# A fused hybrid trunk on one core: scan products of a chunk issued as one burst, squares of the head summed by TensorE, eight early conditioning products

## The chip, the cores and the metric

The kernel runs on one core of one Trainium2 chip. The metric is device time in microseconds (us), the median of several executions; lower is better. The engines are called as in the profile: PE (TensorE, matrix products), PEld (its weight loads), DVE (VectorE), ACT (ScalarE), POOL (GpSimd) and SP (SyncE, which only issues DMAs). Each engine works through its own queue in order, as the kernel's schedule has written it.

## The reference, cut to what matters

One layer over 1024 time steps and 1024 channels, in fp32. `u` is the modulated RMSNorm of the input; the modulation comes from the conditioning vector `c`. One projection of `u` feeds a gated short convolution and a state-space (SSD) mixer with 8 groups of 4 heads; both are merged by gates, followed by an MLP.

```python
mod = (c_act @ w_ada[i] + b_ada[i]).reshape(bsz, N_MOD, D_MODEL)[:, :, None, :]
u = rms_norm(x, ln1[i]) * (1.0 + scale1) + shift1          # rms_norm: x * rsqrt(mean(x*x) + EPS) * w
gl, cb, cc, cx, z, xbc, dt = split(u @ w_in)
xbc = silu(causal_depthwise_conv(xbc, ssm_conv_w) + ssm_conv_b)   # width 4
xs, bs, cs = split(xbc)
# scan over chunks, per group (4 heads share bs and cs):
scores = einsum('btgn,bsgn->btsg', cq, bq)
y_diag = einsum('btsg,btsgr,bsgrp->btgrp', scores, decay, xq)
y_off = einsum('btgn,bgrpn->btgrp', cq, state) * exp(a_cum)[..., None]
new_state = state * exp(a_cum[:, -1])[..., None, None] + einsum('bsgn,bsgr,bsgrp->bgrpn', bq, to_end, xq)
y = (y + d_skip * xs) * silu(z)                             # then a norm per group
x = x + gate1 * (merged @ w_o);  x = x + gate2 * (square(relu(u2 @ w_up)) @ w_down)
```

## The kernel before

Every product in fp32 precision is made of three products of split operands: the high part of the weight with the high and the low part of the activations, and the low part with the high part. A tile of a projection (128 channels by 1024 steps) is `proj`: 8 blocks of 128 inputs by two halves by three products, 48 products of 128x512. Four PSUM banks (`mm`) hold the outputs, so two such tiles at a time.

The order of the work on each engine is set when the kernel is built: a scheduler takes the instructions in the order in which the Python code issues them and moves them by its own estimate of times and by dependencies. `tc.issue_after(x)` adds a dependency of order: what is issued under it stands behind `x`. In the head (the first 105 us or so) the order is pinned to that of the code.

The stages:

- **Head** (0 to about 105 us). The input arrives in two halves of 512 steps (`h` = 0, 1), eight blocks `k` each. `square(h, k)` squares a block on ACT and adds it on DVE to an accumulator (`accs`, tile `sacc`; the squares are `ssq`). `sums(h)` sums over the partitions: for each of four 128-step columns, one product of the accumulator with a column of ones into `st`. A product here is an fp32 one, which PE runs in two passes. `root` turns the sums into 1/sqrt on DVE, `spread` brings that to all partitions with another product. Between these PE works on the first tiles of the projection (`part`, line L402, tiles `mm`, `sx`, `st`).
- **Early projections** (about 105 to 640 us). Conditioning products run on DVE: `gemv` multiplies a 512 KB block of `w_ada` (tile `wv`, loaded by POOL's queue) by the conditioning and sums it (line L323, result `mcol`). `gemvs(n, ...)` does the next n of 32. Ten stand ahead of the projections, three stand ahead of each of the two pairs f = 12 and 14 of the gate tiles, and the others in later loops up to the z tiles. `strassen_pair` (L155 products) does pairs of projection tiles by a Strassen scheme; ACT copies its first result out of PSUM (`cu`, L178).
- **Scan** (about 640 to 1300 us). Eight groups of eight chunks of 128 steps. While `ssd_group(g)` runs its chunks, `proj_group(g+1)` supplies four tiles of the next group: two of `xs`, one of `bf`, one of `cf`. Lines L121, L122 and L124 are their products. `xbc_evac` takes a tile out of PSUM: two copies on ACT into one of two padded tiles (`raw0`, `raw1`, L738), a scaled copy on ACT into `cacc` (L740), three shifted multiply-adds on DVE that read `raw` (the taps of the convolution), tanh on ACT (L743), and a last multiply-add on DVE.
- **Output projections and MLP** (1300 us to the end), which the change does not touch.

One chunk c of the scan has these products on PE:

- **A**: the scores of `cf` and `bf` (L779) and three transposes (L780 to L782). DVE makes `smk` (masked scores), `xd` and `xe` from it.
- **B**: four heads of `xd` times `seg`, in tiles of 64 columns (L802). `seg` is the masked decay: four relus and one exp on ACT from `acb` (a DMA of 256 KB by SP's queue, L777, two buffers), times `smk` on DVE.
- **O**: two products of the state with `cf` into the same PSUM tile (L807), not in chunk 0.
- **C**: the update of the state from `bt` and `xe` (L824), not in the last chunk. DVE adds it to the decayed state.

DVE then scales O (`t`) and adds B, and adds the skip term into `xs` (two multiply-adds of 128x128 a chunk). A has two PSUM tiles, B and C one each. After the last chunk of a group, `xs` is multiplied by the gate (`zs`, two operations of 128x1024), and `finish` squares and sums these for the group's norm.

Of the kernel before, what the change touches and what calls it, by code (L numbers as in the profile page):

```python
# [16 lines left out]
P = 128  # L17
# [21 lines left out]
def hybrid_trunk(tc, xT, par, hrows, crow, wada1, wadak, wada2, win, wdt, wco, wso, wo, wup, wdt_, wdn, out):  # L39
# [3 lines left out]
    def tt(o, a, b, op, eng=dve):  # L43
        return eng.tensor_tensor(out=o, in0=a, in1=b, op=op)  # L44
# [296 lines left out]
    accs = {}  # L341

    def square(h, k):
        sq = p0.tile([P, H], F32, name="ssq" if k else "sacc", bufs=2 if k else 1)
        act.activation(sq, xt[k][h], AF.Square)
        if k:
            tt(accs[h], accs[h], sq, ALU.add)
        else:
            accs[h] = sq

    def scale_of(j):
        stt(s1c[:, j:j + 1], mcol[:, 8 + j:9 + j], 1.0, prm[:, LN1 + j:LN1 + j + 1], ALU.add, ALU.mult)

    st = ps0.tile([P, H], F32, name="st")

    def sums(h):
        for j in range(4):
            pe.matmul(st[:, 4 * h + j:4 * h + j + 1], lhsT=accs[h][:, j * P:j * P + P], rhs=ones[:, 0:1],
                      start=h == j == 0, stop=True, skip_group_check=True)

    def root(h):
        r = rsqrt_eps(p0, st[:, 4 * h:4 * h + 4], 1.0 / T, [P, 4], "nst")
# [55 lines left out]
    for h in (0, 1):  # L418
        act.activation(ct[:, hs[h]], rows_c[h], AF.Tanh, scale=0.5)
        stt(cb[:, hs[h]], ct[:, hs[h]], 1.0, rows_c[h], ALU.add, ALU.mult)  # L420
    sums(0)
    first_col()
    high(0)
    high(1)
# [14 lines left out]
    for j in range(1, KT):  # L439
        scale_col(j)  # L440
        shift_lo(j - 1, 0)
        if j == 1:
            for i in (0, 1, 2):
                part((0,), (0, 1), 0, (i,))
            part((0,), (2,), 0, (0, 1))
        scaled(j, 0)
        gemv(wa[j, 0], j)
        if j == 1:
            load_ada(3)
            low(2)  # L450
            part((0,), (2,), 0, (2,))
            load_f(5)
        if j > 2:
            for k in {3: (0, 1, 2), 4: (3, 4), 5: (5, 6), 6: (7,), 7: ()}[j]:
                square(1, k)
        shift_hi(j, 0)
        if j == 1:
            high(3)
            part((0,), (3,), 0, (0, 1))
            high(4)  # L460
        if j == 2:
            load_ada(4)
            part((1,), range(3), 0)
            part((1,), (3,), 0, (0, 1))
            low(3)
            part((0, 1), (3,), 0, (2,))
            part((0, 1), (4,), 0, (0, 1))
            load_f(6)
            high(5)
        if j == 3:  # L470
            load_ada(5)
            part((2,), range(4), 0)
            part((2,), (4,), 0, (0, 1))
            low(4)
            part((0, 1, 2), (4,), 0, (2,))
            part((0, 1, 2), (5,), 0, (0, 1))
            load_f(7)
        if j == 4:
            load_ada(6)
            part((3,), range(5), 0)  # L480
            part((3,), (5,), 0, (0, 1))
            low(5)
            part((0, 1, 2, 3), (5,), 0, (2,))
            high(6)
            low_by_dma(6)
        if j == 5:
            load_ada(7)
            part((4,), range(6), 0)
            part((0, 1, 2, 3, 4), (6,), 0, (0, 1))
            high(7)  # L490
            low_by_dma(7)
        if j == 6:
            part((5,), range(6), 0)
            sums(1)
            part((5,), (6,), 0, (0, 1))
            part((0, 1, 2, 3, 4, 5), (6,), 0, (2,))
        if j == 7:
            dg = root(1)
            part((6,), range(7), 0)
            keep_rb(spread(dg))  # L500
# [51 lines left out]

    p0d = tc.alloc_tile_pool(name="p0d", bufs=1, reuse_waits="tile")
    p0g = tc.alloc_tile_pool(name="p0g", bufs=1, reuse_waits="tile")
    gemvs(10, p0g, 3)
    wdr = p0d.tile([P, KT, NH], F32, name="wdr")
    sp.dma_start(wdr, wdt)
    wd = p0d.tile([P, KT, 2 * NH], F32R, name="wd")
# [67 lines left out]
    for f in range(8, 16, 2):  # L626
        ts_ = [glp.tile([P, T], F32, name="glt") for _ in (0, 1)]

        def gl_ev(i, h, src):
            act.activation(ts_[i][:, hs[h]], src, AF.Tanh, scale=0.5)  # L630

        if f == 10:
            dt_chain()
        elif f > 10:
            gemvs(3, pe1)
        strassen_pair(pe1, win[f], win[f + 1], X, gl_ev)
        for i in (0, 1):
            act.dma_start(gl_d[f + i], ts_[i])
# [133 lines left out]
    def ssd_group(g, xs, bf, cf, prev):  # L772
        state = None
        for c in range(NC_):
            cs = slice(c * P, c * P + P)
            acb = p2.tile([P, 4, P], F32, name="acb")
            sp.dma_start(acb, ac_d[4 * g:4 * g + 4, cs].partition_broadcast(P))  # L777
            A = psA.tile([P, 512], F32, name="A")
            pe.matmul(A[:, 0:P], lhsT=bf[:, cs], rhs=cf[:, cs], start=True, stop=True)  # L779
            pe.transpose(A[:, 128:256], xs[:, 0, cs], ident)  # L780
            pe.transpose(A[:, 256:384], xs[:, 1, cs], ident)
            pe.transpose(A[:, 384:512], bf[:, cs], ident)  # L782
            smk = p2.tile([P, P], F32, name="smk")
            tt(smk, A[:, 0:P], tri, ALU.mult)
            xd = p2.tile([P, 4, 64], F32, name="xd")
            xq = A[:, 128:384].rearrange("p (r k) -> p r k", r=4)
            tt(xd, xq, dt_t[:, c, 4 * g:4 * g + 4].unsqueeze(2).broadcast_to([P, 4, 64]), ALU.mult)
            if c < NC_ - 1:
                bt = p2.tile([P, P], F32, name="bt")
                act.copy(bt, A[:, 384:512])  # L790
                xe = p2.tile([P, 4, 64], F32, name="xe")
                tt(xe, xq, de_t[:, c, 4 * g:4 * g + 4].unsqueeze(2).broadcast_to([P, 4, 64]), ALU.mult)
            seg = p2.tile([P, 4, P], F32, name="seg")
            for r in range(4):
                hd = 4 * g + r
                act.activation(seg[:, r, :], acb[:, r, :], AF.Relu, bias=acum[:, c, hd:hd + 1], scale=-1.0)
            act.activation(seg, seg, AF.Exp, scale=-1.0)
            tt(seg, seg, smk.unsqueeze(1).broadcast_to([P, 4, P]), ALU.mult)
            Bk = psB.tile([P, 512], F32, name="B")
            for r in range(4):  # L800
                o = 64 * (r % 2)
                pe.matmul(Bk[o:o + 64, P * (r // 2):P * (r // 2) + P], lhsT=xd[:, r, :], rhs=seg[:, r, :],  # L802
                          start=True, stop=True, skip_group_check=True)
            ydv = Bk[:, 0:256].rearrange("p (q t) -> p q t", q=2)
            if c > 0:
                for q in (0, 1):
                    pe.matmul(Bk[:, 256 + P * q:256 + P * q + P],  # L807
                              lhsT=state[:, 2 * q:2 * q + 2, :].rearrange("p r k -> p (r k)"),
                              rhs=cf[:, cs], start=True, stop=True, skip_group_check=True)
                ebc = p2.tile([P, 2, P], F32, name="ebc")  # L810
                for q in (0, 1):
                    act.activation(ebc[64 * q:64 * q + 64], acb[64 * q:64 * q + 64, q::2, :], AF.Exp)
                t1 = p2.tile([P, 2, P], F32, name="t1")
                tt(t1, Bk[:, 256:512].rearrange("p (q t) -> p q t", q=2), ebc, ALU.mult)
                tt(t1, ydv, t1, ALU.add)
                src = t1
            else:
                src = ydv
            for q in (0, 1):
                col = DSK + 2 * g + q  # L820
                stt(xs[:, q, cs], xs[:, q, cs], prm[:, col:col + 1], src[:, q, :], ALU.mult, ALU.add)
            if c < NC_ - 1:
                C = psC.tile([P, H], F32, name="C")[:, 0:256]
                last = pe.matmul(C, lhsT=bt, rhs=xe.rearrange("p r k -> p (r k)"), start=True, stop=True)  # L824
                ns = p2.tile([P, 4, 64], F32, name="state")
                cv = C.rearrange("p (r k) -> p r k", r=4)
                if c == 0:
                    dve.tensor_copy(ns, cv)
                else:
                    tt(ns, state, edec[:, c, 4 * g:4 * g + 4].unsqueeze(2).broadcast_to([P, 4, 64]), ALU.mult)  # L830
                    tt(ns, cv, ns, ALU.add)
                state = ns
            if c == 4 and prev is not None:
                finish(prev, last)
            if c == 5:
                zs = [p2.tile([P, T], F32, name="zs") for _ in (0, 1)]
                for q in (0, 1):
                    sp.dma_start(zs[q], z_d[2 * g + q])
            if c == 6 and g in (5, 7):
                rstd(*{5: (0, 4), 7: (4, 6)}[g])  # L840
            yield
        for q in (0, 1):
            tt(zs[q], xs[:, q, :], zs[q], ALU.mult)
            pool.dma_start(y_d[2 * g + q], zs[q])
        return g, zs
# [422 lines left out]
```

## Time and profile before

| what | value |
|---|---|
| time, median of 3 runs | 2101.52 us (2098.99 to 2104.03) |
| time of the profiled execution | 2104.39 us |
| its span | 2102.6 us |
| PE, DVE, ACT busy over the span | 98%, 71%, 46% |
| head 0 to 105 us: PE busy, granted clock | 95.18 us, 0.93 |
| 105 to 640 us: PE busy of 535 | 528.87 us, clock 1.00 |
| scan 640 to 1300 us: PE, DVE, ACT busy of 660 | 653.11, 482.55, 387.86 us, clock 1.00 |
| 1300 us to the end: PE busy of 802.6 | 790.09 us, clock 0.99 |

In the rows of the timeline the columns are start, duration, engine, line and operation, output and inputs, shapes, count, and in brackets the idle time ahead of it with what ended it. Rows of successive matmuls overlap, since a matmul's end lies behind the start of the next: the time that one takes from the stream is read from start to start. In the groups, after the first bar stand the busy time in us and the mean of one in ns, after the second the idle time of that engine ahead of them and what ended most of it. In the rows of windows stand the window, its length, the busy time of PE, PEld, DVE, ACT and POOL with counts, the granted clock of PE, the share of the DMA engines and GB/s.

### The profile page before, as it was taken

Reading aid. Unit: us, or ns where it says so; the run is one execution under the profiler, and the core shown is the slowest. Engines: PE = TensorE matmul, PEld = TensorE weight load, DVE = VectorE, ACT = ScalarE, POOL = GpSimd, SP = SyncE. Lnnn points to the kernel's source line nnn. Section 1 sums busy time; section 2 is a strip of 40 time slices with the busy share of each in tenths; the row PEclk is TensorE's granted clock in tenths of the full one; section 3 lists DMA queues with packets and bytes.
Section 4 is the critical chain, followed back from the end, with each engine's and each line's share of the span. In section 5 each row is a group of like instructions: output and inputs, shape, how many; then the busy total and the mean of one; then the engine's idle time right before and its main releaser. Section 6 shows DMA issues by size and latency. Waiting matters only on the chain.

```text
span 2102.6 us, 26286 instructions
## 1 busy us (share of the span) xinstructions
PE 2067.2 (98%) x9736; PEld 1693.4 (81%) x9736; DVE 1491.5 (71%) x2348; ACT 962.1 (46%) x1570; POOL 178.2 (8%) x247
## 2 busy tenths in 40 slices
PE   8999999999999999999999999999999999999997
PEld 6878878888887878887788787888888888888887
DVE  8777876776863777777977867936866665658675
ACT  4433333333335676666754541334544454544432
POOL 0010000000001000000000000012000001232213
PEclk8999999999999999999999999999999999999998
DMA  9345543222228454555365779643144447998932
GB/s 326 107 160 184 184 166 121 96 74 71 81 83 252 108 144 128 145 130 127 117 204 205 258 266 338 230 142 115 60 165 165 157 163 261 302 241 253 277 78 81
DMA packets 142578, 355.65 MB, mean 169 GB/s; under 512 B 13505, under 2 KB 48705, under 8 KB 140914
## 3 DMA queue, kind: packets, MB, share of 16 engines
q1 hardware_dynamic: 100002, 206.43, 30.2%
q0 software_dynamic: 27280, 105.39, 17.4%
q10 hardware_dynamic: 15168, 42.15, 5.1%
q8 instruction: 77, 1.26, 0.2%
q14 instruction: 51, 0.42, 0.1%
HBM read 275.08 MB, written 78.84 MB: 168 GB/s over the span
## 4 chain that ended last, share of the span: by engine, by line
PE 75%; issue 14%; DMA 6%; DVE 3%; ACT 1%; POOL 1%; SPq 0%; DVEq 0%; POOLq 0%; ACTq 0%
PE mm L155 30%; PE mm L1161 9%; PE mm L121 9%; PE mm L124 9%; PE mm L122 9%; PE mm L402 2%; PE B L802 1%; PE B L807 1%; DMA wraw<-in_win 1%; DMA wv<-in_wada 1%; DMA dr<-in_wdt_ 1%; PE C L824 1%; POOL wv L550 1%; DMA acb<-ac_d 1%; PE st L402 1%
## 5 line engine op out<-in xcount | busy, mean ns | idle before, releaser
L155 PE MATMUL mm<-t,whi 128*128 128x512 f32 x1168 | 359.3, 389 | 3.8 <-DVE cq L44 3.8
L155 PEld LDWEIGHTS mm<-t,whi 128*128 128x128 f32 x1168 | 218.8, 188 | 50.8 <-DVE cq L44 5.7
L155 PE MATMUL mm<-t,wlo 128*128 128x512 f32 x584 | 226.6, 389 | 0.0
L1161 PE MATMUL mm<-op,whi 128*128 128x512 f32 x672 | 207.1, 389 | 1.2 <-DVE y L47 0.7
L121 PE MATMUL mm<-uh,whi 128*128 128x512 f32 x448 | 177.7, 397 | 1.4 <-ACT raw L738 1.4
L122 PE MATMUL mm<-ul,whi 128*128 128x512 f32 x448 | 177.4, 396 | 0.0
L44 DVE TENSOR_TENSOR wlo<-s,whi 128x1024 fp32r<-128x1024 f32 (+1 forms) x128 | 129.0, 1019 | 67.4 <-ACT whi L160 66.5
L44 DVE TENSOR_TENSOR wlo<-wraw,whi 128x1024 fp32r<-128x1024 f32 (+1 forms) x136 | 144.8, 1065 | 11.7 <-ACT whi L160 5.4
L121 PE MATMUL mm<-ys,whi 128*128 128x512 f32 x384 | 149.3, 393 | 1.5 <-DVE s L44 1.5
L122 PE MATMUL mm<-ys,whi 128*128 128x512 f32 x384 | 150.0, 392 | 0.0
L1161 PEld LDWEIGHTS mm<-op,whi 128*128 128x128 f32 x672 | 126.0, 188 | 28.2 <-ACT whi L1147 2.0
L124 PE MATMUL mm<-uh,wlo 128*128 128x512 f32 x448 | 142.8, 395 | 0.0
L160 ACT CAST whi<-wraw 128x1024 fp32r<-128x1024 f32 x80 | 66.9, 837 | 161.5 <-PE mm L155 143.4
L155 PE MATMUL mm<-s,whi 128*128 128x512 f32 x448 | 138.0, 389 | 0.7 <-ACT cu L178 0.7
L1161 PE MATMUL mm<-op,wlo 128*128 128x512 f32 x336 | 130.7, 389 | 0.0
L160 ACT CAST whi<-s 128x1024 fp32r<-128x1024 f32 x80 | 84.1, 1052 | 99.2 <-PE mm L155 93.1
L155 PEld LDWEIGHTS mm<-t,wlo 128*128 128x128 f32 x584 | 109.6, 188 | 22.9
L124 PE MATMUL mm<-ys,wlo 128*128 128x512 f32 x384 | 125.8, 392 | 0.0
L155 PE MATMUL mm<-uh,whi 128*128 128x512 f32 x312 | 122.4, 392 | 2.4 <-ACT cu L178 2.4
L47 DVE SCALAR_TENSOR_TENSOR y<-mm,mcol,y 128x512 f32<-128x512 f32 (+1 forms) x100 | 69.3, 704 | 76.1 <-PE mm L1161 40.2
L47 DVE SCALAR_TENSOR_TENSOR cacc<-raw,hw,cacc 128x1024 f32<-128x1024 f32 x84 | 107.1, 1278 | 21.3 <-ACT cacc L740 21.0
L155 PE MATMUL mm<-ul,whi 128*128 128x512 f32 x312 | 121.9, 391 | 0.0
(318 smaller groups left out, 4483.0 us busy)
## 6 DMA issues: line engine op xcount, KB each, us to landing
wraw<-in_win SPq DMA_DIRECT2D x83, 512.0 KB, 3.9
dr<-in_wdt_ SPq DMA_DIRECT2D x108, 256.0 KB, 5.2
op_d<-hp POOLq DMA_DIRECT2D x12, 1792.0 KB, 7.1
hr<-op_d POOLq DMA_DIRECT2D x42, 512.0 KB, 6.0
wv<-in_wada POOLq DMA_DIRECT2D x32, 512.0 KB, 4.3
acb<-ac_d SPq DMA_DIRECT2D x64, 256.0 KB, 6.1
wraw<-in_wup SPq DMA_DIRECT2D x32, 512.0 KB, 4.0
wlo<-in_win POOLq DMA_DIRECT2D x28, 512.0 KB, 7.7
```

What stands on the lines that cost most here:

```text
L44: return eng.tensor_tensor(out=o, in0=a, in1=b, op=op)
L47: return dve.scalar_tensor_tensor(out=o, in0=a, scalar=s, in1=b, op0=op0, op1=op1)
L121: pe.matmul(o, lhsT=wh, rhs=h_, start=start, stop=False)
L122: pe.matmul(o, lhsT=wh, rhs=l_, start=False, stop=False)
L124: last_mm[0] = pe.matmul(o, lhsT=wl, rhs=h_, start=False, stop=stop)
L155: last_mm[0] = pe.matmul(o, lhsT=l_[:, s_], rhs=r_, start=first and k == j == 0, stop=k == 3 and j == 2, skip_group_check=True)
L160: act.copy(hi, src)
L402: pe.matmul(sps[f, h], lhsT=w_[f][:, j * P:j * P + P], rhs=v_[j][h], start=j == i == 0, stop=j == KT - 1 and i == 2, skip_group_check=True)
L550: pool.dma_start(w_, wada2[i])
L802: pe.matmul(Bk[o:o + 64, P * (r // 2):P * (r // 2) + P], lhsT=xd[:, r, :], rhs=seg[:, r, :], start=True, stop=True, skip_group_check=True)
L807: pe.matmul(Bk[:, 256 + P * q:256 + P * q + P], lhsT=state[:, 2 * q:2 * q + 2, :].rearrange("p r k -> p (r k)"), rhs=cf[:, cs], start=True ...
L1161: pe.matmul(o, lhsT=l_[:, c_], rhs=t[:, r_, k, :], start=first and k == j == 0, stop=k == 3 and j == 2, skip_group_check=True)
```

## The change

Three parts, in the order of the program:

1. **Head.** In the first half the squares 0 to 5 are still added on DVE; their sum goes through PE as before, and the squares 6 and 7 are summed by PE directly, into the same PSUM columns (12 products for 4). In the second half each of the eight squares goes through PE (32 products for 4), and DVE adds none. DVE has 9 additions fewer in all. The squares of the second half are spread over j = 3 to 6 in pairs; the squares 0, 3 and 6 of it use the one buffer of `sacc`, the others two buffers of `ssq`.
2. **Conditioning products.** Eight of them stand ahead of the projections where ten stood; the pairs f = 12 and 14 get four each for three.
3. **Scan, groups 0 to 5.** C of a chunk is ordered behind its last B or O product, and A of the next chunk behind C (or behind the last B or O product). The products of a chunk thus stand as B, O, C, A(next).

```diff
     def square(h, k):
-        sq = p0.tile([P, H], F32, name="ssq" if k else "sacc", bufs=2 if k else 1)
+        acc = h == k == 0
+        one = acc or h == 1 and k % 3 == 0
+        sq = p0.tile([P, H], F32, name="sacc" if one else "ssq", bufs=1 if one else 2)
         act.activation(sq, xt[k][h], AF.Square)
-        if k:
+        if acc:
+            accs[h] = sq
+        elif h == 0 and k < 6:
             tt(accs[h], accs[h], sq, ALU.add)
+            if k == 5:
+                sums(h, accs[h], True, False)
         else:
-            accs[h] = sq
+            sums(h, sq, h == 1 and k == 0, k == KT - 1)
...
-    def sums(h):
+    def sums(h, sq, first, last):
         for j in range(4):
-            pe.matmul(st[:, 4 * h + j:4 * h + j + 1], lhsT=accs[h][:, j * P:j * P + P], rhs=ones[:, 0:1],
-                      start=h == j == 0, stop=True, skip_group_check=True)
+            pe.matmul(st[:, 4 * h + j:4 * h + j + 1], lhsT=sq[:, j * P:j * P + P], rhs=ones[:, 0:1],
+                      start=first and h == j == 0, stop=last, skip_group_check=True)
...
-    sums(0)
...
-            for k in {3: (0, 1, 2), 4: (3, 4), 5: (5, 6), 6: (7,), 7: ()}[j]:
+            for k in {3: (0, 1), 4: (2, 3), 5: (4, 5), 6: (6, 7), 7: ()}[j]:
                 square(1, k)
...
-            sums(1)
...
-    gemvs(10, p0g, 3)
+    gemvs(8, p0g, 3)
...
-            gemvs(3, pe1)
+            gemvs(4, pe1)
...
+            with tc.issue_after(last.ins) if c and g < 6 else contextlib.nullcontext():
+                pe.matmul(A[:, 0:P], lhsT=bf[:, cs], rhs=cf[:, cs], start=True, stop=True)
+                pe.transpose(A[:, 128:256], xs[:, 0, cs], ident)
...
             for r in range(4):
...
+                last = pe.matmul(Bk[o:o + 64, P * (r // 2):P * (r // 2) + P], lhsT=xd[:, r, :], rhs=seg[:, r, :],
+                                 start=True, stop=True, skip_group_check=True)
...
+                    last = pe.matmul(Bk[:, 256 + P * q:256 + P * q + P],
...
             if c < NC_ - 1:
                 C = psC.tile([P, H], F32, name="C")[:, 0:256]
-                last = pe.matmul(C, lhsT=bt, rhs=xe.rearrange("p r k -> p (r k)"), start=True, stop=True)
+                with tc.issue_after(last.ins) if g < 6 else contextlib.nullcontext():
+                    last = pe.matmul(C, lhsT=bt, rhs=xe.rearrange("p r k -> p (r k)"), start=True, stop=True)
```

How this moves instructions is seen best at three places. In these rows the number behind a name tells one buffer or tile of that name from another.

The first is PE's queue where group 1 ends and group 2 begins. Before, the chunk 0 of group 2 is `B_6036`, and the C behind it, `C_6084`, is that of chunk 1; `A_6133` is of chunk 3 of the group:

```order
L802 MATMUL B_6036<-seg_6029,xd_6023 64x128 x4
L824 MATMUL C_6084<-xe_6060,bt_6058 128x256
L779 MATMUL A_6133<-cf_5749,bf_5748 128x128
L780 MATMUL A_6133<-ident_73,xs_5747 128x128
L781 MATMUL A_6133<-ident_73,xs_5747 128x128
L782 MATMUL A_6133<-ident_73,bf_5748 128x128
L121 MATMUL mm_6571<-uh40_139,whi_6566 128x512
L122 MATMUL mm_6571<-ul40_141,whi_6566 128x512
L121 MATMUL mm_6572<-uh41_140,whi_6566 128x512
L122 MATMUL mm_6572<-ul41_142,whi_6566 128x512
```

After, `mm_7082` and `mm_7083` are a tile of the projection for group 4; `B_5755` is the last chunk of group 1, `B_6063` chunk 0 and `B_6096` chunk 1 of group 2:

```order
L124 MATMUL mm_7083<-uh71_161,wlo_7079 128x512
L807 MATMUL B_5755<-seg_5748,xd_5746 64x128 x4
L812 MATMUL B_5755<-cf_5160,state_5734 128x128 x2
L807 MATMUL B_6063<-seg_6056,xd_6050 64x128 x4
L830 MATMUL C_6070<-xe_6054,bt_6052 128x256
L784 MATMUL A_6076<-cf_5776,bf_5775 128x128
L785 MATMUL A_6076<-ident_73,xs_5774 128x128
L786 MATMUL A_6076<-ident_73,xs_5774 128x128
L787 MATMUL A_6076<-ident_73,bf_5775 128x128
L807 MATMUL B_6096<-seg_6089,xd_6083 64x128 x4
L812 MATMUL B_6096<-cf_5776,state_6072 128x128 x2
L830 MATMUL C_6111<-xe_6087,bt_6085 128x256
```

Before, C and A run one and two chunks ahead of B, and projection products follow at once. After, the order is strict, and behind these rows A, B, O, C and A of the next chunk follow before the next projection product: 22 rows in a row, `B_5755` to `A_6160`, without one. The same stands at the borders into groups 4 and 5, and a row of one chunk less at the border into group 3; at the borders into groups 1 and 6 there are bursts with projection products between them.

The second is DVE's queue at the same place. `cacc_6584` (after) and `cacc_6557` (before) are the convolution of the tile `bf` for group 3; its taps read `raw0`, into which the next tile's PSUM banks are then copied. Before:

```order
L44 TENSOR_TENSOR state_6086<-C_6084,state_6086 128x256
L47 SCALAR_TENSOR_TENSOR xs_6363<-xs_6363,cacc_6491 128x1024
L44 TENSOR_TENSOR smk_6138<-A_6133,tri_74 128x128
L47 SCALAR_TENSOR_TENSOR cacc_6557<-raw0_4794,hw_105,cacc_6557 128x1024
L44 TENSOR_TENSOR seg_6104<-seg_6104,smk_6096 128x512
L44 TENSOR_TENSOR xe_6102<-A_6091,de_t_102 128x256
L47 SCALAR_TENSOR_TENSOR cacc_6557<-raw0_4794,hw_105,cacc_6557 128x1024
L44 TENSOR_TENSOR zs_5664<-zs_5664,zs_5665 128x1024
L44 TENSOR_TENSOR xd_6140<-A_6133,dt_t_101 128x256
L44 TENSOR_TENSOR t1_6079<-B_6069,ebc_6076 128x256
L44 TENSOR_TENSOR state_6128<-state_6086,edec_104 128x256
L47 SCALAR_TENSOR_TENSOR cacc_6557<-raw0_4794,hw_105,cacc_6557 128x1024
```

After:

```order
L44 TENSOR_TENSOR state_6113<-C_6111,state_6113 128x256
L47 SCALAR_TENSOR_TENSOR cacc_6584<-raw0_4821,hw_105,cacc_6584 128x1024
L44 TENSOR_TENSOR state_6155<-state_6113,edec_104 128x256
L44 TENSOR_TENSOR smk_6123<-A_6118,tri_74 128x128
L44 TENSOR_TENSOR xd_6125<-A_6118,dt_t_101 128x256
L47 SCALAR_TENSOR_TENSOR cacc_6584<-raw0_4821,hw_105,cacc_6584 128x1024
L47 SCALAR_TENSOR_TENSOR cacc_6650<-raw1_4822,hw_105,cacc_6650 128x1024
L44 TENSOR_TENSOR seg_6131<-seg_6131,smk_6123 128x512
L44 TENSOR_TENSOR zs_5691<-zs_5691,zs_5692 128x1024
L44 TENSOR_TENSOR xe_6129<-A_6118,de_t_102 128x256
L47 SCALAR_TENSOR_TENSOR cacc_6584<-raw0_4821,hw_105,cacc_6584 128x1024
```

The operations are nearly the same. Before, the first tap stands behind rows that need `C_6084` and `A_6133`, which PE's queue has at once behind `B_6036`, and the third behind one that needs `B_6069`. After, the first tap stands behind a row that needs `C_6111`, the C of chunk 1, and the others behind rows that need `A_6118` (`smk_6123`, `xd_6125`, `xe_6129`), which PE's queue has only behind that C.

The third is PE's queue at the start of the head. `st<-ones` are the sums, `mm<-ccol` the first conditioning column, `st<-sdg` the spreading of the root. Before:

```order
L289 MATMUL mm<-crw,ones 128x512 x2
L285 MATMUL mm<-ones 128x128 x9
L358 MATMUL st<-ones,sacc 128x1 x4
L339 MATMUL mm<-ccol,wk 128x1 x8
L369 MATMUL st<-sdg,ones 128x512
```

After:

```order
L285 MATMUL mm<-ones 128x128 x9
L364 MATMUL st<-ones,sacc 128x1 x4
L364 MATMUL st<-ones,ssq 128x1 x8
L339 MATMUL mm<-ccol,wk 128x1 x8
L375 MATMUL st<-sdg,ones 128x512
```

The eight products of the squares 6 and 7 stand behind the four of the accumulator. Later in the head, where the second half had one row of four products, there are now 32 products in seven rows between the products of `part`.

More of the change, by code (lines that the diff above doesn't have):

```diff
@@ L778, in ssd_group @@
             A = psA.tile([P, 512], F32, name="A")
[L779 to L782, printed above, removed]
+            with tc.issue_after(last.ins) if c and g < 6 else contextlib.nullcontext():
+                pe.matmul(A[:, 0:P], lhsT=bf[:, cs], rhs=cf[:, cs], start=True, stop=True)
+                pe.transpose(A[:, 128:256], xs[:, 0, cs], ident)
+                pe.transpose(A[:, 256:384], xs[:, 1, cs], ident)
+                pe.transpose(A[:, 384:512], bf[:, cs], ident)
             smk = p2.tile([P, P], F32, name="smk")
@@ L801, in ssd_group @@
                 o = 64 * (r % 2)
-                pe.matmul(Bk[o:o + 64, P * (r // 2):P * (r // 2) + P], lhsT=xd[:, r, :], rhs=seg[:, r, :],
-                          start=True, stop=True, skip_group_check=True)
+                last = pe.matmul(Bk[o:o + 64, P * (r // 2):P * (r // 2) + P], lhsT=xd[:, r, :], rhs=seg[:, r, :],
+                                 start=True, stop=True, skip_group_check=True)
             ydv = Bk[:, 0:256].rearrange("p (q t) -> p q t", q=2)
@@ L806, in ssd_group @@
                 for q in (0, 1):
-                    pe.matmul(Bk[:, 256 + P * q:256 + P * q + P],
-                              lhsT=state[:, 2 * q:2 * q + 2, :].rearrange("p r k -> p (r k)"),
-                              rhs=cf[:, cs], start=True, stop=True, skip_group_check=True)
+                    last = pe.matmul(Bk[:, 256 + P * q:256 + P * q + P],
+                                     lhsT=state[:, 2 * q:2 * q + 2, :].rearrange("p r k -> p (r k)"),
+                                     rhs=cf[:, cs], start=True, stop=True, skip_group_check=True)
                 ebc = p2.tile([P, 2, P], F32, name="ebc")
```

## The prediction

> **What bounds the kernel now.** I read the page first, then the stages, PE's waits, PE's timeline around single chunks, and the groups of DVE and ACT by form.
>
> ```profile
> span 2102.6 us, 26286 instructions
> PE 2067.2 (98%) x9736; PEld 1693.4 (81%) x9736; DVE 1491.5 (71%) x2348; ACT 962.1 (46%) x1570; POOL 178.2 (8%) x247
> 690.00:990.00 300.00, 300.00 (x1632) 241.39 (x1632) 225.69 (x431) 206.20 (x415) 21.80 (x28) 1.00 0.53 131
> ```
>
> PE is busy 98% of the span. The third row is a stretch of the scan (columns: length, then PE, PE's weight loads, DVE, ACT, POOL, then granted clock): PE never stops in 300 us, while DVE is busy 75% and ACT 69%. So time is PE work plus PE idle, and a change counts only as it alters one of these. PE's waits between 640 and 1300 us (total, times, longest) are short:
>
> ```profile
> PE C L824 <- DVE xe L44: 2.0, 2, 1.3
> ...
> PE mm L121 <- ACT raw L738: 1.4, 1, 1.4
> ...
> PE B L802 <- DVE t L44: 0.8, 1, 0.8
> ```
>
> **Part 1, the scan's bursts: what merging saves.** One chunk that stands together in the kernel before, and one whose B is split by C (start, duration):
>
> ```profile
> 705.00 0.39 PE L121 MATMUL mm<-uh,whi 128*128 128x512 f32 x1
> 705.32 0.66 PE L802 MATMUL B<-seg,xd 128*64 128x128 f32 x8
> 705.91 0.71 PE L807 MATMUL B<-cf,state 128*128 128x128 f32 x4
> 706.46 0.60 PE L824 MATMUL C<-xe,bt 128*128 128x256 f32 x2
> 706.89 0.38 PE L779 MATMUL A<-cf,bf 128*128 128x128 f32 x2
> ...
> 707.67 0.40 PE L121 MATMUL mm<-uh,whi 128*128 128x512 f32 x1
> ```
> ```profile
> 783.21 0.43 PE L802 MATMUL B<-seg,xd 128*64 128x128 f32 x2
> 783.57 0.70 PE L824 MATMUL C<-xe,bt 128*128 128x256 f32 x2
> 784.20 0.65 PE L802 MATMUL B<-seg,xd 128*64 128x128 f32 x6
> 784.78 0.73 PE L124 MATMUL mm<-uh,wlo 128*128 128x512 f32 x2
> 785.36 0.39 PE L121 MATMUL mm<-uh,whi 128*128 128x512 f32 x1
> 785.59 0.40 PE L122 MATMUL mm<-ul,whi 128*128 128x512 f32 x1
> ```
>
> By starts, unsplit B takes 0.59 (705.32 to 705.91), O 0.55, C 0.43, A with its transposes about 0.5. The split B with C takes 1.57 (783.21 to 784.78) against 0.59 + 0.43 = 1.02: a split costs 0.55. The order before has 11 of them in groups 0 to 5, the one after none: 11 x 0.55 = 6, taken as -5 (0 to -6, as some are cut by a single product). The three longest waits above, 1.3 + 1.4 + 0.8 = -3.5, can go (0 to -3.5). Nothing else is saved: the same products run in either order.
>
> **What the tie costs.** In most places 30 to 45 projection products, some 7 us and more at the 0.23 us from one to the next (785.36 to 785.59), stand between two bursts and hide DVE's path from A to the next B; there the tie costs nothing. At four group boundaries (into groups 2, 3, 4, 5) nothing stands between: projection has run ahead, and the product that follows the train writes PSUM whose last content must first be copied into a raw buffer that DVE still reads. In DVE's queue that reading (third tap on `cacc_6584`, after) stands behind rows that need B, C and A of the train itself. So PE must go step by step with DVE. The prices of DVE's rows, 690 to 990 us (busy, mean ns):
>
> ```profile
> L47 DVE SCALAR_TENSOR_TENSOR cacc<-raw,hw,cacc 128x1024 f32<-128x1024 f32 x57 | 72.6, 1277 | 5.3 <-ACT cacc L740 5.2
> L44 DVE TENSOR_TENSOR seg<-seg,smk 128x512 f32<-128x512 f32 x36 | 24.6, 684 | 6.6 <-ACT seg L797 6.4
> L47 DVE SCALAR_TENSOR_TENSOR xs<-xs,prm,t 128x128 f32<-128x128 f32 x66 | 20.0, 344 | 0.2
> L44 DVE TENSOR_TENSOR xd<-A,dt_t 128x256 f32<-128x256 f32 x36 | 15.1, 420 | 20.8 <-PE B L802 20.6
> L44 DVE TENSOR_TENSOR t<-B,ebc 128x256 f32<-128x256 f32 x32 | 13.4, 420 | 4.7 <-PE B L807 4.7
> ...
> L44 DVE TENSOR_TENSOR smk<-A,tri 128x128 f32<-128x128 f32 x37 | 10.5, 284 | 9.1 <-PE A L782 9.1
> L47 DVE SCALAR_TENSOR_TENSOR xs<-xs,cacc 128x1024 f32<-128x1024 f32 x8 | 9.7, 1218 | 2.5 <-ACT xs L743 2.5
> ...
> L44 DVE TENSOR_TENSOR zs<-xs,zs 128x1024 f32<-128x1024 f32 x8 | 9.4, 1216 | 0.0
> ```
> ```profile
> L796 ACT ACTIVATE seg<-acb,acum 128x128 f32<-128x128 f32 x144 | 46.0, 392 | 37.4 <-PE B L802 37.4
> ...
> L740 ACT ACTIVATE cacc<-raw,hb,hw 128x1024 f32<-128x1024 f32 x19 | 23.5, 1236 | 2.8 <-DVE bf L47 2.8
> ...
> L738 ACT COPY raw<-mm 128x512 f32<-128x512 f32 x40 | 21.3, 581 | 0.0
> ...
> L850 ACT ACTIVATE zs<-zs 128x1024 f32<-128x1024 f32 x8 | 8.5, 1057 | 5.6 <-DMA y_d<-zs 5.6
> ```
>
> The train into group 2, with 0.42 for every 128x256 operation:
> - O(1.7) to B(2.1): DVE does t twice (0.84), four small xs (1.38), two zs (2.43), the state's copy and scaling (0.84), smk, xd, seg (1.39): 6.9 us. PE has B, C and A of chunk 0, 1.5 us. Idle 5.4 by the means; back-to-back DVE rows start a little before the one ahead ends, so I take 4.5.
> - C(2.1) needs xe, behind two large xs: 2 x 1.22 + 0.42 = 2.9 against B and O, 1.1. Idle 1.7.
> - A(2.2) to B(2.2): t twice, two small xs, two state operations, smk, xd, three taps of cacc (3.8), seg: 7.6 us against 0.9 of C and A. Idle 6 to 6.7; I take 6.
> - C(2.2) needs xe behind the zs sum: 1.64 against 1.1, idle 0.5.
> - The product after the train: third tap 1.28 and one or two raw copies of 0.58, against C and A 0.9: idle 1 to 1.5.
>
> That is 14. ACT can add to the third step: the load of acb for the chunk ahead starts only when an older seg has read its buffer, and four relus of 0.39, the zs square of 1.06 and the cacc activation of 1.24 come between it and DVE's taps, 3.9 in all, of which half is taken: 16 a train (10 where DVE is ahead on arrival and no ACT row delays it; 20 with all of ACT's and the load's lateness). On SP's queue the loads of later projection weights stand behind a late acb; a tile's 48 products last 48 x 0.23 = 11 us, which hides that, so I put nothing on it (uncovered, it is in the 20). The train into group 3 is a chunk shorter but ends on the same raw copy: 14. Sum 3 x 16 + 14 = +62 (40 to 80).
>
> **The clock.** Two consecutive windows of the kernel before:
>
> ```profile
> 132.84:136.25 3.41, 1.15 (x9) 0.96 (x8) 3.11 (x6) 0.92 (x3) 0.00 (x0) 1.00 0.22 90
> 136.25:139.66 3.41, 3.32 (x8) 2.64 (x9) 3.23 (x6) 2.32 (x5) 0.00 (x0) 0.50 0.11 14
> ```
>
> PE was busy 1.15 of 3.41 us, and the clock of the next 3.41 us was 0.50: some 1.5 us of work lost. A train has idle stretches of 4.5 and 6, so one or two such windows: about 2 each, +8 (0 to 14). [...]
>
> **Part 2, the head.**
>
> ```profile
> 13.37 1.87 PE L358 MATMUL st<-ones,sacc 128*128 128x1 f32 x8 [3.04 <-DVE sacc L44]
> ...
> 48.96 0.50 PE L402 MATMUL mm<-ul,whi 128*128 128x512 f32 x1 [0.63 <-DVE ul L47]
> ...
> 59.34 0.94 PE L358 MATMUL st<-ones,sacc 128*128 128x1 f32 x8
> ```
> ```profile
> PE sx L402 <- DVE wlx L44: 0.6, 2, 0.3
> ```
>
> A sum is 4 products of two passes, 0.94/8 = 0.12 a pass at most, less where the last one's end overlaps the next start. Second half: 64 passes instead of 8, 56 x 0.11 = +6.2 (5.6 to 6.7 at 0.10 to 0.12). DVE loses seven adds there, so its waits of 0.63 and 0.6 go, -1.2 (0 to -1.2); the first sum may wait for its square, +0.5 (0 to 1). First half: 16 more passes, 0.23 each by the second row, 3.7, but the sum starts two adds of DVE earlier (0.69 each) and the last two squares need none; part runs before the clock drops: +0.25 (0 to 1.8). ACT's squares keep their number. Together +5.7.
>
> **Part 3, eight early gemvs.**
>
> ```profile
> 134.38 1.28 DVE L323 CUSTOM_DVE_ANT_0 wv<-wv,cb,prm 128x1024 f32<-128x1024 f32 x1
> ```
> ```profile
> 135.70 0.58 ACT L178 COPY cu<-mm 128x512 f32<-128x512 f32 x1 [1.31 <-DVE mcol L323]
> ```
> ```profile
> 136.34 0.80 PE L155 MATMUL mm<-uh,whi 128*128 128x512 f32 x1 [2.35 <-ACT cu L178]
> ```
>
> PE's 2.35 here waits for ACT's cu, which waits for the mcol of the tenth gemv. Two gemvs fewer (2.6 of DVE, and their loads) take the chain away: -2.35 and the half clock behind it, -1.5; together -3.9 (0 to -3.9). The two go to two later f pairs, with two wv loads on POOL's queue: between nothing and one pair not hidden, 2.6; taken +1.
>
> **Sum**: 62 + 8 - 5 - 3.5 + 5.7 - 3.9 + 1 = +64.3 on the profiled execution's 2104.39 (span 2102.6, 1.8 around it), which is 2.9 above the median 2101.52 of the runs. So 2104.4 + 64.3 - 2.9 = 2166.
>
> **The rivals.**
> - *Short trains*: DVE arrives ahead, 10 each and no clock loss: 40 - 5.7 = +34; 2136. For it: ACT and DVE have idle time before a boundary. Against: the order of DVE's queue.
> - *Long trains*: 80 + 14, head 3 more: 2193. For it: acb's loads would come late at each train.
> - *The other side, faster*: DVE's rows that I count in the trains are done before PE arrives, because PE does longer projection runs just ahead. It needs PE to come 7 us behind DVE at each boundary; below 1.4 us idle a train it decides (5.7/4). Then -5 - 3.5 + 5.7 - 3.9 + 1 = -5.7: 2096. Against: DVE's rows wait for B and C of the same train, which a head start does not supply.
> - *No change*: trains of 1 to 2 us cancel these gains: about 2102.
>
> **How the numbers follow.** Forecast 0.67 (2150 to 2182), short trains 0.13, long 0.09, other side 0.08, no change 0.03. Of 2137 to 2195 outside lie the last two and half of the short trains. About 0.2%, 4.2 us, is what a measurement of this kernel can tell: faster 0.08, same 0.03, slower 0.89.
>
> **What the profile after would show.** Right: PE waits at C for xe, at B for seg, at the projection's first product for the raw copy, in sums of 10 or more at each of four boundaries between about 750 and 1200 us, with a low granted clock right behind; B never split; 64 passes of st in the head; no wait of 2.35 near 136 us. Wrong: PE at 300 of 300 us through the scan as before, or gaps at one boundary alone. What would upset it most: a DVE row order at run time whose waits I misread, so that the taps do not stand behind the train.

## The result and the profile after

The changed kernel takes 2174.32 us (median; 2172.88 to 2176.58) against 2100.26 for the kernel before on the same chip: ratio 1.0357, 95% interval 1.0341 to 1.0373. That is 74 us slower; the forecast was 2166, 64 us slower. The profiled execution's span is 2174.8 us, 72.2 above that of before.

The page, two windows of the scan, and PE's longest waits in the scan (total, times, longest):

```profile
span 2174.8 us, 26435 instructions
...
PE 2091.1 (96%) x9808; PEld 1715.7 (79%) x9808; DVE 1486.3 (68%) x2339; ACT 966.8 (44%) x1570; POOL 178.5 (8%) x247
```
```profile
690.00:990.00 300.00, 270.66 (x1432) 218.64 (x1430) 183.74 (x360) 177.17 (x351) 19.62 (x25) 0.94 0.45 111
990.00:1240.00 250.00, 222.17 (x1149) 179.14 (x1148) 187.46 (x351) 137.88 (x272) 5.24 (x9) 0.92 0.47 149
```
```profile
PE B L807 <- DVE seg L44: 38.7, 7, 10.3
PE mm L121 <- ACT raw L742: 11.8, 3, 11.1
...
PE C L830 <- DVE xe L44: 2.7, 5, 1.2
```

Where PE had been busy 300 of 300 us, it now stands for 29, at a granted clock of 0.94. The waits are for seg (the path from A to B), for the raw copy, and for xe. In what follows a chunk is written with its group: B(2.1) is the B of chunk 1 in group 2; a border is the place where one group ends and the next begins.

To place the loss I compare the start of the same product in both traces, counting PE's matmuls in order but for A, B, O, C and the sums:

| product | before | after | difference so far |
|---|---|---|---|
| 300th, end of the head | 87.94 | 93.05 | +5.1 |
| 600th, behind the wait at 136 us | 158.89 | 162.66 | +3.8 |
| 1250th, behind the z stage | 311.26 | 313.76 | +2.5 |
| 2800th, start of the scan's projection | 661.69 | 664.19 | +2.5 |
| 5200th, scan over | 1363.97 | 1433.06 | +69.1 |
| last | 2095.28 | 2167.07 | +71.8 |

The scan stretch (2800th to 5200th) can be split further: PE's waits of over 0.1 us; the time that a granted clock below 1 cost (the share missing from 1, times PE's busy time in those stretches); and what is left, the products themselves. The edits of e1 to e11 are told below.

| kernel | stretch | waits | clock | rest |
|---|---|---|---|---|
| before | 702.3 | 6.9 | 0.0 | 695.4 |
| after | 768.9 | 59.6 | 16.8 | 692.5 |
| e1, ties alone | 779.6 | 66.3 | 20.9 | 692.4 |
| e4, C's tie without A's | 721.0 | 20.9 | 6.8 | 693.4 |
| e8, A's tie without C's | 778.0 | 58.1 | 29.7 | 690.2 |
| e3, both ties, even spread | 736.6 | 31.7 | 12.9 | 692.0 |
| e5, e3 with finish's sums in A's tiles | 732.5 | 29.8 | 11.4 | 691.4 |
| e10, e3 without C's tie | 725.6 | 21.4 | 13.1 | 691.0 |
| e7, e5 without C's tie | 698.8 | 7.2 | 1.7 | 689.9 |
| e11, e7 spread another way | 722.7 | 22.5 | 8.4 | 691.8 |

The border into group 2, PE's rows with a wait (the bracket holds the idle time and what ended it), and the DVE and ACT rows behind the longest:

```profile
830.42 0.66 PE L807 MATMUL B<-seg,xd 128*64 128x128 f32 x8 [1.07 <-ACT seg L801]
...
835.65 0.66 PE L807 MATMUL B<-seg,xd 128*64 128x128 f32 x8 [3.40 <-DVE seg L44]
...
838.17 1.22 PE L830 MATMUL C<-xe,bt 128*128 128x256 f32 x2 [1.17 <-DVE xe L44]
...
846.94 1.12 PE L807 MATMUL B<-seg,xd 128*64 128x128 f32 x8 [6.48 <-DVE seg L44]
...
851.23 0.50 PE L121 MATMUL mm<-uh,whi 128*128 128x512 f32 x1 [0.37 <-ACT raw L742]
```
```profile
841.65 1.28 DVE L47 SCALAR_TENSOR_TENSOR cacc<-raw,hw,cacc 128x1024 f32<-128x1024 f32 x1 [1.76 <-ACT cacc L744]
```
```profile
838.03 1.28 ACT L801 ACTIVATE seg<-acb,acum 128x128 f32<-128x128 f32 x4 [2.01 <-DMA acb<-ac_d]
```

These are the prediction's steps in their order: 1.07 ahead of B(2.0) and 3.40 ahead of B(2.1), 1.17 for C(2.1), 6.48 for B(2.2), and 0.37 at the product behind the row; 12.5 together. The borders into groups 3, 4 and 5 have 15.8, 15.4 and 13.5 in the same way, 57.2 in all. At the border into group 3 the long step is 11.07, and its cause is one more link:

```profile
928.95 0.79 PE L121 MATMUL mm<-uh,whi 128*128 128x512 f32 x1 [11.07 <-ACT raw L742]
```
```profile
918.18 1.06 ACT L856 ACTIVATE zs<-zs 128x1024 f32<-128x1024 f32 x1 [4.78 <-DMA y_d<-zs]
```
```profile
920.41 1.28 DVE L47 SCALAR_TENSOR_TENSOR cacc<-raw,hw,cacc 128x1024 f32<-128x1024 f32 x1 [4.54 <-ACT cacc L744]
```

`finish` squares zs in place, and must wait until the DMA that stores it has read it; the cacc activation stands behind that square on ACT, DVE's first tap behind the activation, and PE's row of products behind the tap. ACT waits for that store at the borders into groups 4 and 5 too (4.59 and 3.17).

### The profile page after: what moved, and what is told of

The parts are those of the page before. It is cut to its first block, busy times and chain, and to the rows that moved or that the text cites. A ratio compares the mean times of both kernels' runs of the same rounds, so it can differ in the third digit from the quotient of the medians.

```text
span 2174.8 us, 26435 instructions
## 1 busy us (share of the span) xinstructions
PE 2091.1 (96%) x9808; PEld 1715.7 (79%) x9808; DVE 1486.3 (68%) x2339; ACT 966.8 (44%) x1570; POOL 178.5 (8%) x247
## 4 chain that ended last, share of the span: by engine, by line
PE 73%; issue 15%; DMA 6%; DVE 3%; ACT 2%; POOL 1%; SPq 0%; DVEq 0%; POOLq 0%; ACTq 0%
PE mm L155 29%; PE mm L1167 9%; PE mm L121 9%; PE mm L122 9%; PE mm L124 9%; PE mm L408 2%; DMA y_d<-zs 1%; PE st L408 1%; DMA dr<-in_wdt_ 1%; PE sx L408 1%; PE B L807 1%; PE B L812 1%; DMA y<-x_d 1%; PE C L830 1%; DVE cacc L47 1%
## 5 line engine op out<-in xcount | busy, mean ns | idle before, releaser
L801 ACT ACTIVATE seg<-acb,acum 128x128 f32<-128x128 f32 x256 | 81.9, 390 | 101.7 <-PE B L807 94.3
```

## Experiments

Each kernel was timed beside runs of the kernel before on the same chip (2100.0 to 2100.8 us).

**e1: the ties alone.** Head and conditioning products as before.

> Only the scan's ties; head and conditioning products as before. Theory (trains at four group borders, where PE goes step by step with DVE): the scan alone carries the loss, 66.6 us between the start and the end of the scan in the changed kernel's trace, so 2100 + 67 = 2167 (2160 to 2172; one of the four rows is a chunk part shorter here). Rival (the head's 56 further passes and the earlier end of the conditioning products shift the scan's start and so make the rows late): below 2150.

Measured: 2180.8, ratio 1.0376 (1.0350 to 1.0403). The ties carry the whole loss. The time is 9 above the range that was given: 8.0 us of waits stand outside the borders here, near 1264 and 1279 us, and the clock cost 4.1 more. That the rows depend on where the head ends is refuted: without its 2.5 us the borders' waits are no shorter (57.4 against 57.2).

**e2, e6, e12: the other parts.** e2 is the changed kernel without ties; e6 has only `gemvs(8, ...)` and `gemvs(4, ...)`; e12 only the head's sums.

> The head's sums on PE and the 8 early conditioning products, without the scan's ties. Theory: the stages do not meet; the head costs 5.1, the wait near 136 us gives back 1.3, the z stage 1.3: +2.5, so 2103 (2100 to 2106). Rival (freed DVE time pays later, or the moved products delay the scan): outside of that, 2098 or less, or 2108 or more.

> Only the eight early conditioning products (ten before, later pairs four for three); head and scan as before. Theory: 1.4 of the wait near 136 us and the half clock behind it go (2.9 in the run without ties), and 1 to 2.7 in the z stage: 2100.5 - 4.5 = 2096 (2094 to 2098). Rival (the wait only moves, or the z stage pays it back): 2099 or more.

> Only the head's sums on PE. Theory: 5.1 us at the end of the head in the changed kernel's trace, from 56 passes more and a later clock rise or not: 2104 to 2107. Rival (the nine additions that DVE saves pay for the passes): 2102 or less.

Measured: e2 2102.0, ratio 1.0004 (0.9990 to 1.0018); e6 2099.6, ratio 0.9990 (0.9977 to 1.0002); e12 2104.1, ratio 1.0020 (1.0003 to 1.0036). e2 and e12 lie in their ranges: the head's sums cost about 4 us, and the two parts together make no difference that can be told. e6 missed its range by 1.6 and came out at the rival's figure; whether the eight products gain at all stays inside the uncertainty.

**e4 and e8: one tie of the two.**

```diff
-            with tc.issue_after(last.ins) if c and g < 6 else contextlib.nullcontext():   # e4: A free
+            with contextlib.nullcontext():
...
-                with tc.issue_after(last.ins) if g < 6 else contextlib.nullcontext():     # e8: C free
+                with contextlib.nullcontext():
```

> The changed kernel without the tie of A (C still stands behind its own B or O, the head and the conditioning products as changed). A runs ahead again; one border (into group 4) still has chunks 0 to 2 without a projection product between. Theory (the tie of A puts DVE's path from A to B on PE's path; C's alone gives a train that waits only for xe and B's operands made ahead): one train at 5 to 10, the head's 2.5, splits of B gone -3: 2104 to 2112. Rival (C's tie is what makes the rows, through the state): 2140 or more.

> The changed kernel without the tie of C: A still stands behind C of the chunk ahead, C may move. Four borders have two or three chunks without a projection product. Theory (A's tie puts the path from A over smk, xd and seg to B on PE's path at the borders): 2150 to 2170, near the changed kernel. Rival (C's tie, whose removal of the other one left 2124, is the larger part): 2125 or less.

Measured: e4 2124.3, ratio 1.0114 (1.0086 to 1.0143); e8 2179.9, ratio 1.0370 (1.0331 to 1.0409). PE's waits of e4, then of e8:

```profile
PE A L784 <- DVE xe L44: 16.6, 4, 6.0
```
```profile
PE B L807 <- DVE seg L44: 18.9, 6, 4.3
PE mm L121 <- ACT raw L742: 14.6, 4, 4.5
PE C L830 <- DVE xe L44: 11.1, 5, 4.5
```

A's tie alone makes the rows at the borders, and alone costs as much as both. But C's tie alone is not free, as I had thought: A, which runs two chunks ahead, waits for the buffer that xe still reads. That xe stands late in DVE's queue because C is late is my reading; no run sets it apart. Both expectations were too low, by 12 and by 10.

**e3: both ties, the projection held back.** In the changed kernel seg is ready long before B in a group's middle (chunk 4 of group 1):

```profile
790.98 0.38 PE L784 MATMUL A<-cf,bf 128*128 128x128 f32 x2
```
```profile
793.24 0.68 DVE L44 TENSOR_TENSOR seg<-seg,smk 128x512 f32<-128x512 f32 x1
```
```profile
798.43 0.66 PE L807 MATMUL B<-seg,xd 128*64 128x128 f32 x8
```

From A to the end of seg it is 2.9 us, and B stands 4.5 us later, with projection products between that the borders lack. So block k of projection tile i for group G was put behind the burst of chunk 2i + k/4 + 1 of group G-2, which leaves 24 products between any two bursts:

```diff
+            m_ = marks.get(n + k // 4 + 1)     # n = 8 * (G - 2) + 2 * i; marks: last product of a chunk's burst
+            with tc.issue_after(m_) if m_ is not None else contextlib.nullcontext():
                 mm3(ps, wh[:, c0:c0 + P], wl[:, c0:c0 + P], ...)
```

> All of the scan's ties in groups 0 to 5, and the projection held back: block k of tile i of group G stands behind the burst of chunk 2i + k/4 + 1 of group G-2, so that 24 projection products stand between any two bursts and no border is without them. Head and conditioning products as before. Theory (the loss comes from projection running ahead in the groups' middles, where seg is ready 4.5 us before B in the changed kernel, so that nothing is left for the borders): the loss goes, and with no B split and no wait of the scan left the time is 2092 to 2100. Rival (the strict order itself exposes DVE's path from A to B in every chunk): 24 products last 5.5 us, waits of 1 us or more a chunk remain and the time stays above 2130.

Measured: 2138.9, ratio 1.0178 (1.0157 to 1.0200). Half of the loss goes and no wait for seg is left, but C now waits in every group:

```profile
PE C L831 <- ACT row L868: 13.9, 4, 4.3
PE C L831 <- DVE xe L44: 10.4, 6, 3.0
PE C L866 <- ACT row L868: 7.5, 4, 1.9
```

So the uneven spread is one cause, not the only one. The new waits are for the single PSUM bank that C shares with the sums of `finish`, whose copy (`row`) stands in ACT's queue (at chunk 5 of groups 1 to 4, where these sums stand), and for xe.

**e5, e10, e7: the bank and C's tie.** e5 is e3 with finish's sums in a tile of A; e10 is e3 without C's tie; e7 has both edits.

```diff
-            ps = psC.tile([P, H], F32, name="C")      # in finish; e5 and e7
+            ps = psA.tile([P, H], F32, name="A")
```

> The ties with 24 projection products between bursts (as the run before), and the sums of finish written into a tile of A (two buffers) in place of the one bank that they share with C. Theory (what was left of the loss there is mostly that bank: C waits for the copy of finish's row out of it, 13.9 and 7.5 us in all, and the clock falls behind each): these 21.4 go and about 7 of the 12.9 that the clock cost, 2139 - 28 = 2111 (2104 to 2118); the waits of C for xe, 10.4, stay. Rival (the copies only stood where ACT or DVE would have held the burst anyway): 2125 or more.

> As the run with C free and 24 projection products between bursts, but with finish's sums in the bank that they share with C, as in the kernel before. Theory (with C free the shared bank binds no burst, since C is issued a few us ahead of B): 2098 to 2104. Rival (C waits for the row's copy as it did with C tied, 21.4 us): 2115 or more.

> As the run with finish's own bank, without the tie of C: A still stands behind C, but C may stand ahead of B. Theory (the waits of C for xe exist because C must stand right behind B and O, while xe stands behind taps in DVE's queue): they shrink, 2098 to 2105. Rival (A, which still stands behind C, waits for the same rows): 2109 or more.

Measured: e5 2135.9, ratio 1.0172 (1.0143 to 1.0202); e10 2126.3, ratio 1.0118 (1.0092 to 1.0145); e7 2098.3, ratio 0.9994 (0.9977 to 1.0012). Waits of e5, e10 and e7:

```profile
PE C L831 <- DVE xe L44: 20.9, 10, 3.0
...
PE B L808 <- DVE seg L44: 5.3, 4, 1.3
```
```profile
PE C L831 <- ACT row L868: 15.5, 4, 4.1
```
```profile
PE C L831 <- DVE xe L44: 4.1, 4, 1.4
...
PE B L808 <- DVE seg L44: 2.4, 3, 1.1
```

e5 came 25 above its forecast: the waits for the bank went, and waits for xe and seg took their place. The time is that of the rival that was written down, but its reason (ACT and DVE would have been late there anyway) is not shown, since the edit moved A too. The sums now take one of A's two tiles, and A(2.5), which stood 24 products ahead of B(2.5) in e3, stands between them and right ahead of B(2.5):

```profile
849.35 0.40 PE L866 MATMUL A<-sqh,onec 128*128 128x512 f32 x1
849.58 0.38 PE L785 MATMUL A<-cf,bf 128*128 128x128 f32 x2
...
849.94 0.48 PE L867 MATMUL A<-sql,onec 128*128 128x512 f32 x1
...
851.84 0.66 PE L808 MATMUL B<-seg,xd 128*64 128x128 f32 x8 [1.31 <-DVE seg L44]
...
855.63 0.70 PE L831 MATMUL C<-xe,bt 128*128 128x256 f32 x2 [2.50 <-DVE xe L44]
```

This comes at chunk 5 of groups 1 to 4 and makes 15.2 of the 29.8 us of waits. e10 missed too: with C free the bank still holds it. Only both edits together bring the time back to that of before, as expected for e7. So with the even spread, the shared bank and C's tie both had to go before PE ran through again, with A's tie still in place. Whether the uneven spread had to go as well is not tested with these two edits; e8 had C free at that spread and no wait for the row's copy, and lost as much as both ties.

**e9: the square apart.** One of finish's two squares goes to a tile of its own.

> The changed kernel with the first of finish's two squares written to a tile of its own, so that it need not wait for the DMA that still writes zs out. Theory (at the borders into groups 3 and 4 ACT stands 4.8 us for that DMA, and DVE's first tap 4.5 us behind it, which the prediction had not in its sum): the long step there shrinks from 11.1 and 10.3 to about 6.5, and the whole by 9 plus some clock: 2160 to 2166. Rival (acb's load or the second square, which still waits, holds the tap as long): 2171 or more.

Measured: 2179.2, ratio 1.0381 (1.0356 to 1.0405): no gain. The first square waits for no store now, and the long step at the border into group 3 fell from 11.1 to 5.4 (forecast: about 6.5). But that into group 2 rose from 6.5 to 9.9 and that into group 4 stayed at 10.1: ACT waits at both for acb's load (3.06 and 3.95 us), which was the rival. The four borders' waits fell by 4.5 in all, and waits elsewhere rose by more (11.3 against 2.4). What the DMA link alone costs stays open.

**e11: what the runs spoke for.** e7 with the eight conditioning products, and each projection block held one chunk longer (`+ 2` for `+ 1`; the expectation's "lead of one chunk more" should have said one less).

> Everything that the runs spoke for: A's tie, C free, the projection spread with a lead of one chunk more (22 to 26 products between bursts where the run e7 had 15 to 38), finish's own bank, eight early conditioning products, head as before. Theory: e7's waits in the scan of 7 us halve and the splits' 5.5 stay saved, the conditioning products give 1 to 3: 2093 (2090 to 2097). Rival (the waits follow ACT's and DVE's queues and stay): 2097 or more, no difference that can be told.

Measured: 2117.4, ratio 1.0092 (1.0070 to 1.0115), a miss. B waits for seg, 2.6 us at each of four places:

```profile
PE B L808 <- DVE seg L44: 11.9, 5, 2.6
```

These are not the borders but chunk 5 of groups 1 to 4, as in e5: A(2.5) stands between finish's two sums and right ahead of B(2.5), and DVE does two taps of the convolution (1.28 and 1.27) between this A and the end of seg:

```profile
832.42 0.38 PE L785 MATMUL A<-cf,bf 128*128 128x128 f32 x2
```
```profile
834.07 1.27 DVE L47 SCALAR_TENSOR_TENSOR cacc<-raw,hw,cacc 128x1024 f32<-128x1024 f32 x1
835.26 0.68 DVE L44 TENSOR_TENSOR seg<-seg,smk 128x512 f32<-128x512 f32 x1
```

In e7 B waits 1.08 at two of these places. Another 6.6 us of waits, which e7 has not, are at a later sum of `finish` (4.07) and at a product of a later stage (2.53). No kernel of this study is clearly faster than the one before.

## Why the prediction was right, and where its terms were off

- **Mechanism and place: right.** e1 shows that the ties carry the loss; the trace shows it at the four borders, in the steps and for the tiles that were named. The measured time is 8 above the forecast and inside the likeliest case's own range (2150 to 2182). That the total came so near is in part luck: terms missed in both directions, the clock by +9, the rows by -5. Terms of 1 to 3 us are read from one trace each and mean little where other traces of the same code differ by as much.
- **Waits of the rows, +62: measured 57.2.** The first step came out as forecast (1.07 + 3.40 against 4.5), though the 1.07 waits for ACT's part of seg and not for DVE; the third was 6.5 against 8 with half of ACT's part, in group 2, where acb's load was late by 2.0 as allowed for; the last two steps nearly vanished. The store of zs, which was not in the sum, made up for that at groups 3 to 5.
- **Clock, +8: measured 16.8, the worst of the sizes.** I counted one or two slow windows of 3.41 us a border. There are four into group 2 (836.8 to 850.4 us) and six into each of groups 3, 4 and 5. What the term had wrong is the way back: the clock stayed low as long as the step-by-step work left PE idle. In these rows the clock stands third from the end:

```profile
829.95:833.37 3.42, 1.83 (x15) 1.40 (x15) 3.38 (x6) 3.40 (x12) 1.41 (x2) 1.00 0.65 169
833.37:836.78 3.41, 1.13 (x12) 0.97 (x12) 3.41 (x9) 2.65 (x5) 0.55 (x1) 1.00 0.94 199
836.78:840.19 3.41, 2.24 (x9) 1.71 (x7) 3.03 (x7) 2.04 (x5) 0.00 (x0) 0.50 1.02 381
840.19:843.61 3.42, 0.26 (x2) 0.00 (x0) 1.96 (x4) 3.41 (x6) 0.00 (x0) 0.50 0.08 24
843.61:847.02 3.41, 0.08 (x2) 0.12 (x4) 3.41 (x5) 1.60 (x3) 0.00 (x0) 0.50 0.14 33
847.02:850.43 3.41, 3.41 (x17) 2.90 (x18) 3.41 (x4) 2.47 (x6) 0.00 (x0) 0.50 0.56 172
850.43:853.84 3.41, 3.04 (x15) 2.36 (x14) 3.41 (x6) 3.18 (x7) 0.00 (x0) 1.00 0.06 25
```

  Here the windows at 0.50 in which PE was busy for 2.24, 0.26 and 0.08 us were followed by another at 0.50, and the one with 3.41 us by one at 1.00. That a window slowed by the wait ahead is broken by the next wait, and so slows the one behind it, is my reading of these rows.

- **Splits, -5: measured -2.9** (rest 695.4 to 692.5). The count was wrong: the order before splits B seven times in groups 0 to 5, not eleven, and three times in groups 6 and 7, where the change leaves them. Seven by 0.55 are 3.9. In e7, which has none of the ten, the rest is 5.5 lower, just 10 x 0.55; e8 and e11 have none either and are 5.2 and 3.6 lower, with more clock loss to take off. So a split costs 0.36 to 0.55, and the price was right or somewhat high.
- **Scan's old waits, -3.5: about -4.5.** Outside the borders 2.4 us (59.6 - 57.2) are left of 6.9. But e2, e6 and e12, whose scan is that of before, have 3.3 to 4.7 in this stretch, so that the trace of before had more of them than the others, and part of this is chance.
- **Head, +5.7: measured +5.1.** The 64 passes take 6.9 us where eight took 0.8, as was said, and one sum waits for its square:

```profile
11.56 1.05 PE L364 MATMUL st<-ones,sacc 128*128 128x1 f32 x8 [1.01 <-DVE sacc L44]
12.48 2.02 PE L364 MATMUL st<-ones,ssq 128*128 128x1 f32 x16
...
37.53 1.05 PE L364 MATMUL st<-ones,sacc 128*128 128x1 f32 x8 [0.80 <-ACT sacc L347]
```

- **136 us, -3.9: measured -1.3.** The gemv is gone from the chain, but the wait only shrank to 0.95, and in this trace a slow window follows it still (140.46 to 143.88 us, clock 0.50). The step that failed is "takes the chain away": behind the gemv stood another, from PE's own last small product over ACT's copies of z and cu (0.37 and 0.59). The 2.35 was also more than usual: the wait is 0.95 in all seven traces with eight gemvs there, but with ten it is 0.95 in e1, e10 and e12 and up to 2.35 in the others, the longest in the profile of before:

```profile
140.05 0.50 PE L155 MATMUL mm<-uh,whi 128*128 128x512 f32 x1 [0.95 <-ACT cu L178]
```
```profile
139.14 0.37 ACT L579 COPY z<-st 128x256 f32<-128x256 f32 x1 [3.02 <-PE st L576]
139.41 0.59 ACT L178 COPY cu<-mm 128x512 f32<-128x512 f32 x1
```

- **z stage, +1: measured -1.3.** No cost of the fourth gemv shows, and no gain can be told: from the 600th to the 1250th product it is 149.5 to 155.1 us in the seven traces with ten gemvs and 148.5 to 152.4 in the seven with eight.
- **After the scan, nothing: measured +2.7** in this trace, where the clock lost 3.7 us there against 0.3 before; no run ties this to the change, and the other twelve traces take 729.6 to 739.3 us there (before 731.3, after 734.0).
- **What the prediction did not see:** that C's tie has a price of its own. e4 and e5 show it: 22 us with A free (e4 against e2), 38 between e5 and e7. In the changed kernel it lies hidden in the same waits, since A's tie alone (e8) costs as much as both.

At the borders the clock was already at 0.50 before the long steps of 6.5 to 11.1 us began: at group 2 it fell 1.1 us behind the step of 3.40, and at groups 3 to 5 it fell 2.2 to 2.5 us into that step. In e11 two of the four gaps of 2.6 us, at 836 and 902 us, were followed by a window at 0.50 and two were not: their windows held 1.49 and 0.77 us of PE's work against 1.85 and 1.95. Outside the scan the gap of 2.35 us that ended at 136.34 us before the change, and that of 0.95 us that ended at 140.05 us after it, each led into a window at 0.50.

## What to carry to other kernels

An order that a scheduler chose is not only a list of positions but a reserve of independent work; fixing a small part of it moves that reserve. Before tying instructions into a burst, look for the places where the other queue that the burst depends on has nothing left to cover it (here: projection used up in the groups' middles, where operands were 4.5 us early, and missing at the borders), and walk step by step through both queues there with durations from the trace. And where a tile or PSUM bank is shared with rare work (here finish's sums, first in C's bank and then in A's tiles), a strict order can turn that sharing into a wait in every round: in e3 C waited 13.9 us in four places for the copy of these sums.

## What the runs showed of the hardware

The granted clock fell beside waits of under 3 us too (2.6 us in e11, 2.35 at 136 us before the change, 0.95 at 140 us after it), but not beside each. In the scan, with waits of at most 1.44 us (e7), the clock lost 1.7 us in 699 us; e11's scan, with four waits of 2.6 among others, lost 8.4; e3's and e5's, with waits of 1.3 to 4.3 in pairs some 4 us apart, 12.9 and 11.4. In the changed kernel's scan the clock was at 0.50 in four stretches, one at each border: 836.8 to 850.4, 911.9 to 932.4, 993.8 to 1014.3 and 1075.7 to 1096.2 us. What decides whether it falls is not shown. In this kernel PE was busy for 1.83 us of the window of 3.42 us that ended at 833.37 us, and the next one was at 1.00; it was busy for 2.46 us of the window of 3.41 us that ended at 140.46 us, with the wait of 0.95 us in it, and the next one was at 0.50, a loss of about 1.7 us. In e2 and e6 no slow window followed the same wait.
